# A decoder step on one core: the four output tiles of q made side by side while x and the weights arrive

## The chip, the cores and the metric

The kernel runs on one core of one Trainium2 chip. The metric is device time of one execution in microseconds (us); lower is better. A core has five engines that run beside each other and meet at semaphores: TensorE (PE in the profile, PEld for its weight loads), VectorE (DVE), ScalarE (ACT), GpSimd (POOL) and SyncE (SP, which here only issues transfers). ScalarE and GpSimd can issue transfers too.

## What is computed

One layer of a hybrid decoder, for 256 prompt tokens and 32 sample tokens (N = 288 columns). Cut to what matters here:

```python
def rms_norm(x, g):
    return x * rsqrt(mean(x * x, axis=-1) + EPS) * g

z = rms_norm(x, ln1) @ w_in                   # 288 x 1024 times 1024 x 2560
u, va, q, k, vb = split(z, ...)               # 512 columns each
q = rms_norm(q.reshape(8 heads, 64), q_norm)  # k likewise
mix = concat(spatial_gate(u, va), block_sparse_attention(q, k, vb, paged cache))
h = x + mix @ w_out
h = h + square(relu(rms_norm(h, ln2) @ w_up)) @ w_down
y = h + sigmoid(rms_norm(h, ln3) @ w_ple_gate) * rms_norm(p @ w_ple_proj, ple_norm)
```

The row factor of the first `rms_norm`, 1/sqrt(mean of squares), is called `r1` below. It is a factor per token, so the kernel multiplies it in after the matrix product.

## The kernel before

All activations lie with features on the 128 partitions and the 288 tokens along the free axis. A weight matrix comes as chunks of 128 x 1024 floats (512 KB). In the input projection a chunk holds one output tile: eight blocks of 128 x 128, one for each k, the 128 input features that a block contracts over. Chunks 0 to 3 make q, 4 to 7 k, 8 to 11 v, 12 to 15 u, 16 to 19 a.

Every product is made in three passes of a reduced format (`mm3`, lines 220 to 223). ScalarE rounds a weight to `hi` (line 132), VectorE makes the rest `lo` = raw - hi (line 139); x goes the same way into `Ah` (ScalarE, line 230) and `Al` (VectorE, line 231, an operation on h and Ah with ln1 as a scalar). The passes are hi Ah (L221), hi Al (L222) and lo Ah (L223). A chunk is 8 k times 3 passes, 24 matrix products. There are four buffers for raw chunks and three for `hi` and for `lo`: chunk c+4 is loaded when `lo` of c is done, and chunk c+3 can be rounded when TensorE has done with c.

At the start SP loads x in four pieces of two k each and the first chunks. TensorE begins with nine products of ones that nobody reads (line 296). Then chunk 0 goes over all eight k, then chunk 1, and so on. The squares of x for `r1` are two GpSimd products, two ScalarE squares, one GpSimd sum and three VectorE sums (lines 330 to 341); a product with ones (`stat`, line 235) sums them over the partitions, and `rsqrt_act`, `rsqrt_dve` make `r1` of it. Each tile of q leaves PSUM by a multiplication with `r1` (line 375), is squared (line 377), summed by heads (L235 again) and scaled.

The program text gives an order by turns (`ORDER`, `step`): in a turn w a chunk is used, in a turn T a tile of the paged cache. Such a tile is eight pages of 256 KB. For the first two tiles all eight are issued by SP. A turn T of the first kind multiplies q with the keys of one tile: 16 small products of 32 output rows (line 543). A scheduler then fixes each engine's order ahead of time, so the text's order is not kept to the letter: key products are put between products of chunks. On the chip every engine keeps its fixed order and waits where something is late.

Of the kernel before, what the change touches and what calls it, by code (L numbers as in the profile page):

```python
# [10 lines left out]
AF = mybir.ActivationFunctionType  # L11
# [3 lines left out]
N = 288  # L15
# [20 lines left out]

# w: next chunk of weights, T: next tile of cached pages, G: group of the spatial gate, A: head pair of the prompt's
# attention, m: masks, P: input of the layer embedding, s and S: stores, -: a turn without matrix products of its own
ORDER = (
    "w w w w - w w w m T T T w w w w w w w w T w w - w w w T - T G G s T G A G T w T T T A A - A - T w - "  # L40
    "T T w w T T P w S w w w w w"
# [4 lines left out]
def tile_decode_step(ctx: ExitStack, tc: tile.TileContext, w, xT, pT, kT, vP, pt, vec, const, aws, abd, abs_,  # L46
# [27 lines left out]

# [1 line left out]
    pt_sb = stile([1, 64], "pt", dt=I32)  # L76
# [7 lines left out]
    pool.dma_start(pt_sb, pt)  # L84
    act.dma_start(vec_sb, vec)
    dve.memset(ones, 1.0)
# [19 lines left out]

# [1 line left out]
    h = stile([128, 8, N], "h")  # L108
# [5 lines left out]

# [1 line left out]
    NW = w.shape[0]  # L116
    raw, hi, lo = {}, {}, {}

    def load_w(c, parts=1):
        if c >= NW or c in raw:  # L120
            return
        raw[c] = stile([128, 1024], "raw", NRAW)
        n = 1024 // parts
        for i in range(parts):
            sp.dma_start(raw[c][:, n * i:n * i + n], w[c][:, n * i:n * i + n])
# [16 lines left out]

    # pages are asked for at the pace of the arithmetic, so that weights don't queue behind them
    pace = {"pe": 0.0, "dma": 0.0, "page": 0, "used": 0, "w": 6, "split": 2, "wn": 0}

# [17 lines left out]

# [1 line left out]
    pending = []  # L165
# [14 lines left out]
    def step(unit=None, weights=None, us=2.95):  # L180
        """One turn of the pipeline. A generator that yields n goes on n turns later, with those that read PSUM;
        n + 0.5: with those that need PE, after them; 0: at the end of this turn."""
        if weights is not None:
            pace["wn"] = weights
            for c in range(pace["split"], weights + 1):
                load_w(c)
                split_hi(c)
                split_lo(c)
                pace["split"] = c + 1
        ahead = [c for c in range(pace["split"], pace["wn"] + 3) if c in raw]  # L190
        for c in ahead:
            split_hi(c)
            pace["split"] = c + 1
        for q in pending:
            q[0] = max(q[0] - 1, 0)
        due(0)
        due(1)
        if unit is not None:
            resume(unit)
        for c in ahead:  # L200
            split_lo(c)
        # the second half of w_out waits for the last page
        for c in range(pace["w"], pace["split"] + NRAW):
            if c in raw or c >= NW:
                pace["w"] = c + 1
            elif c < W_HOLD or pace["page"] >= PAGE_HOLD:
                load_w(c)
                pace["w"] = c + 1
                pace["dma"] += 1.46
            else:  # L210
                break
        load_pages(us)
        due(2)
# [4 lines left out]

# [1 line left out]
    def mm3(out, wh, wl, xh, xl, start, stop):  # L220
# [4 lines left out]
    def split(dh, dl, src, scale=None):  # L225
        if scale is None:
            act.activation(dh, src, AF.Copy)
            dve.tensor_tensor(dl, src, dh.bitcast(F32), OP.subtract)
        else:
            act.activation(dh, src, AF.Copy, scale=scale)  # L230
            dve.scalar_tensor_tensor(dl, src, scale, dh.bitcast(F32), OP.mult, OP.subtract)  # L231
# [6 lines left out]
    def rsqrt_act(ss, count):  # L238
        """first guess of 1/sqrt(ss/count + eps), its square, and -(ss/count + eps)/2"""
        y, v, y2 = tmp(), tmp(), tmp()  # L240
        act.activation(y, ss, AF.Abs_reciprocal_sqrt, bias=eps, scale=1.0 / count)
        act.activation(v, ss, AF.Identity, bias=heps, scale=-0.5 / count)
        act.activation(y2, y, AF.Square)
        return y, v, y2
# [5 lines left out]
    def g_rstd(name, acc):  # L250
        t = rsqrt_act(stat(acc, ones), D)
        yield 0
        st[name] = stile([128, N], "rs", 2)
        rsqrt_dve(st[name], *t)
# [9 lines left out]

# [1 line left out]
    def load_x(i):  # L266
        sp.dma_start(h[:, 2 * i:2 * i + 2], xT[:, 2 * i:2 * i + 2])

    load_x(0)
    load_w(0, 2)  # L270
    load_x(1)
    load_x(2)
    load_x(3)
    load_w(1, 2)
    load_w(2)
    load_w(3)
    sp.dma_start(cst, const)
# [5 lines left out]

    def split_x(i):
        for k in range(2 * i, 2 * i + 2):
            split(Ah[:, k], Al[:, k], h[:, k], ln1(k))

    def split_w(c, parts=1):
        n = 1024 // parts
        for i in range(parts):  # L290
            split_hi(c, n * i, n * i + n)
            split_lo(c, n * i, n * i + n)

    warm = misc_ps()
    for _ in range(NWARM):
        pe.matmul(warm[:, 0:128], lhsT=ones, rhs=ones, start=True, stop=True)
    split_x(0)
    split_w(0, 2)
    split_x(1)
    split_x(2)  # L300
    split_x(3)
    load_w(4)
    split_w(1, 2)
    load_w(5)

# [1 line left out]
    def load_p():  # L307
# [21 lines left out]

    def g_x():  # L330
        sq = [sqx[i // 2][:, 2 * (i % 2):2 * (i % 2) + 2] for i in range(4)]
        for i in range(4):
            x = h[:, 2 * i:2 * i + 2]
            if i < 2:
                pool.tensor_tensor(sq[i], x, x, OP.mult)
            else:
                act.activation(sq[i], x, AF.Square)
        pool.tensor_tensor(sq[0], sq[0], sq[1], OP.add)
        dve.tensor_tensor(sq[2], sq[2], sq[3], OP.add)
        dve.tensor_tensor(sq[0], sq[0], sq[2], OP.add)  # L340
        dve.tensor_tensor(xacc, sq[0][:, 0], sq[0][:, 1], OP.add)
        yield 1.5
        yield from g_rstd("r1", xacc)

    resume(g_x())

    def g_embed():
# [15 lines left out]

# [1 line left out]
    def in_tile(c, name, tag):  # L365
# [5 lines left out]
    def u_qk(c, name, tag, g):  # L371
        p = k8(c, Ah, Al, s_ps() if c == 1 else None)
        yield 3 if c == 0 else 2
        j, dst = in_tile(c, name, tag)
        dve.tensor_tensor(dst, p, st["r1"], OP.mult)
        sq = tmp()
        act.activation(sq, dst, AF.Square)
        yield 2.5 if c in (2, 3) else 1.5
        t = rsqrt_act(stat(sq, blk), 64)
        yield 0  # L380
        r = tmp()
        rsqrt_dve(r, *t)
        dve.scalar_tensor_tensor(dst, dst, g, r, OP.mult, OP.mult)
        if name == "q":
            for hh in range(2):
                pp = slice(64 * hh, 64 * hh + 64)
                src = dst[pp, NP:N].rearrange("p (b q) -> p b q", b=8)
                if hh:
                    act.activation(Qb[pp, j, :, :, 2 * j + hh], src, AF.Copy)
                else:  # L390
                    dve.tensor_copy(Qb[pp, j, :, :, 2 * j + hh], src)

    def nat(src, dst_p, dst_s):
        """src [128 feat, 288 tokens] -> dst_p [128 tokens, 2, 128 feat], dst_s [32 tokens, 128 feat]"""
        p = misc_ps()
        for c in range(2):
            pe.transpose(p[:, 128 * c:128 * c + 128], src[:, 128 * c:128 * c + 128], ident)  # L397
        pe.transpose(p[0:NS, 256:384], src[:, NP:N], ident)
        act.activation(dst_p, p[:, 0:256].rearrange("p (c f) -> p c f", c=2), AF.Copy)
        act.activation(dst_s, p[0:NS, 256:384], AF.Copy)  # L400
# [51 lines left out]

# [1 line left out]
    def u_g(g):  # L454
# [17 lines left out]

# [1 line left out]
    def u_A(j):  # L474
# [56 lines left out]

# [1 line left out]
    def u_K(t):  # L533
# [98 lines left out]

# [1 line left out]
    def u_out(c, half, i):  # L634
# [27 lines left out]

# [1 line left out]
    mask_r = stile([128, 256], "maskr", dt=F32R)  # L664
# [22 lines left out]

    wn, kn, cnt = 0, 0, {"G": 0, "A": 0}
    for op in ORDER:
# [21 lines left out]

# [1 line left out]
    hid = []  # L713
# [151 lines left out]
```

## Time and profile before

| | us |
|---|---|
| median of 3 executions | 427.66 (427.47 to 428.17) |
| span of the profiled execution, first to last instruction | 425.1 |
| median minus span: what lies around the span | 2.5 |
| TensorE busy in the span | 414.2 (97%) |
| VectorE, ScalarE, GpSimd busy | 270.0, 206.9, 41.5 |

The profile gives one execution on one core, by its span; the executions that were timed are longer by what lies before the first and after the last instruction. Busy time of TensorE includes the modelled end of each product, so products that follow each other overlap: one lasts 0.29 us, but the next starts after 0.13 us. Times in the rows below count from the start of the span. L12 is line 12 of the kernel, and buffer numbers are left out of names: `raw`, `hi`, `lo` as above, `h` is x, `mm`, `S` and `misc` are PSUM tiles, `T` are shared work tiles, `kv` are cache pages.

### The profile page before, as it was taken

To read this page: it belongs to the slowest core of one execution; us is meant where nothing else is said; L and a number is where in the kernel's file an instruction comes from. 1 tells how busy PE (TensorE), PEld (TensorE's weight loads), DVE (VectorE), ACT (ScalarE), POOL (GpSimd) and SP (SyncE) were. 2 spreads that over 40 slices of the span, in tenths; PEclk is the share of its full clock that TensorE was granted. 3 is DMA by queue.
4 is the path that set the end of the run, shared out by engine and by line. 5 is a ranking of instruction groups with operands and counts; after the bars stand their busy time and mean duration, and the time that the engine had idled before them with its cause. 6 is when DMAs were issued, how large, how long until landed. Compare 5 with 4: busy or idle time off the path is not lost.

```text
span 425.1 us, 8557 instructions
## 1 busy us (share of the span) xinstructions
PE 414.2 (97%) x3100; PEld 371.2 (87%) x3100; DVE 270.0 (64%) x485; ACT 206.9 (49%) x370; POOL 41.5 (10%) x65
## 2 busy tenths in 40 slices
PE   5999999999999999998999999999999999999995
PEld 4997869893575584998999999999999999999995
DVE  4788434657546563597999978777435445435773
ACT  6587325767252353666555445444333343343631
POOL 5401211103113220041000000000000000000000
PEclk9899999999999999999999999999999999999999
DMA  8999994888899688943454545445445455455411
GB/s 269 323 307 351 395 392 158 284 294 306 295 310 311 219 283 310 324 161 126 172 170 154 173 155 188 154 159 188 150 166 180 150 168 178 147 183 167 159 47 56
DMA packets 33963, 92.29 MB, mean 217 GB/s; under 512 B 4753, under 2 KB 6049, under 8 KB 33921
## 3 DMA queue, kind: packets, MB, share of 16 engines
q1 hardware_dynamic: 28944, 77.52, 52.6%
q0 software_dynamic: 3824, 12.34, 8.1%
q10 hardware_dynamic: 1152, 1.89, 1.3%
q8 instruction: 24, 0.39, 0.4%
q14 instruction: 19, 0.15, 0.1%
HBM read 89.31 MB, written 2.42 MB: 216 GB/s over the span
## 4 chain that ended last, share of the span: by engine, by line
PE 93%; DVE 3%; DMA 1%; issue 1%; ACT 1%; SPq 0%; DVEq 0%
PE mm L221 24%; PE mm L222 24%; PE mm L223 24%; PE S L543 5%; PE S L615 4%; PE misc L235 2%; PE misc L480 1%; DMA h<-xT 1%; PE misc L527 1%; DVE T L231 1%; DVE lo L139 1%; PE misc L516 1%; PE misc L483 1%; PE misc L397 1%; PE misc L458 1%
## 5 line engine op out<-in xcount | busy, mean ns | idle before, releaser
L132 ACT ACTIVATE hi<-raw 128x1024 fp32r<-128x1024 f32 (+1 forms) x104 | 108.4, 1043 | 131.2 <-PE mm L222 104.1
L139 DVE TENSOR_TENSOR lo<-raw,hi 128x1024 fp32r<-128x1024 f32 (+1 forms) x104 | 125.0, 1202 | 59.9 <-ACT hi L132 58.2
L221 PE MATMUL mm<-T,hi 128*128 128x288 f32 x296 | 87.9, 298 | 0.2 <-ACT T L230 0.2
L222 PE MATMUL mm<-T,hi 128*128 128x288 f32 x296 | 86.7, 293 | 1.2 <-DVE T L231 1.2
L221 PE MATMUL mm<-Ah,hi 128*128 128x288 f32 x280 | 85.9, 307 | 1.5 <-ACT Ah L230 0.8
L223 PE MATMUL mm<-T,lo 128*128 128x288 f32 x296 | 86.8, 294 | 0.0
L222 PE MATMUL mm<-Al,hi 128*128 128x288 f32 x280 | 84.8, 303 | 1.9 <-DVE Al L231 1.9
L223 PE MATMUL mm<-Ah,lo 128*128 128x288 f32 x280 | 83.6, 299 | 0.4 <-DVE lo L139 0.4
L221 PE MATMUL mm<-kv,hi 128*128 128x288 f32 x224 | 66.1, 295 | 0.0
L222 PE MATMUL mm<-kv,hi 128*128 128x288 f32 x224 | 66.0, 295 | 0.0
L223 PE MATMUL mm<-kv,lo 128*128 128x288 f32 x224 | 65.9, 294 | 0.0
L222 PEld LDWEIGHTS mm<-Al,hi 128*128 128x128 f32 x280 | 53.3, 190 | 5.7 <-issue 3.1
L221 PEld LDWEIGHTS mm<-Ah,hi 128*128 128x128 f32 x280 | 53.1, 190 | 5.2 <-issue 2.9
L222 PEld LDWEIGHTS mm<-T,hi 128*128 128x128 f32 x296 | 55.6, 188 | 1.6 <-DVE T L231 1.5
L221 PEld LDWEIGHTS mm<-T,hi 128*128 128x128 f32 x296 | 55.5, 188 | 0.5 <-ACT T L230 0.4
L223 PEld LDWEIGHTS mm<-T,lo 128*128 128x128 f32 x296 | 55.4, 187 | 0.0
L223 PEld LDWEIGHTS mm<-Ah,lo 128*128 128x128 f32 x280 | 53.3, 190 | 1.7 <-issue 1.0
L222 PEld LDWEIGHTS mm<-kv,hi 128*128 128x128 f32 x224 | 42.3, 189 | 0.0
L223 PEld LDWEIGHTS mm<-kv,lo 128*128 128x128 f32 x224 | 42.3, 189 | 0.0
L221 PEld LDWEIGHTS mm<-kv,hi 128*128 128x128 f32 x224 | 42.0, 188 | 0.0
L543 PE MATMUL S<-kv,T 128*32 128x256 f32 x256 | 24.3, 384 | 0.0
L736 DVE TENSOR_TENSOR tmp<-mm,rs 128x288 f32<-128x288 f32 x32 | 14.6, 456 | 10.8 <-PE mm L223 10.7
(193 smaller groups left out, 446.8 us busy)
## 6 DMA issues: line engine op xcount, KB each, us to landing
raw<-w SPq DMA_DIRECT2D x100, 512.0 KB, 3.3
kv<-kT SPq DMA_DIRECT2D x46, 256.0 KB, 4.8
kv<-vP SPq DMA_DIRECT2D x31, 256.0 KB, 4.5
kv<-vP POOLq DMA_DIRECT2D x27, 256.0 KB, 5.5
kv<-kT POOLq DMA_DIRECT2D x18, 256.0 KB, 5.5
kv<-vP ACTq DMA_DIRECT2D x6, 256.0 KB, 5.2
h<-xT SPq DMA_DIRECT2D x4, 288.0 KB, 5.2
raw<-w SPq DMA_DIRECT2D x4, 256.0 KB, 5.3
```

What stands on the lines that cost most here:

```text
L132: act.activation(hi[c][:, a:b], raw[c][:, a:b], AF.Copy)
L139: dve.tensor_tensor(lo[c][:, a:b], raw[c][:, a:b], hi[c][:, a:b].bitcast(F32), OP.subtract)
L221: pe.matmul(out, lhsT=wh, rhs=xh, start=start, stop=False)
L222: pe.matmul(out, lhsT=wh, rhs=xl, start=False, stop=False)
L223: pe.matmul(out, lhsT=wl, rhs=xh, start=False, stop=stop)
L231: dve.scalar_tensor_tensor(dl, src, scale, dh.bitcast(F32), OP.mult, OP.subtract)
L235: pe.matmul(p[:, :N], lhsT=lhsT, rhs=src, start=True, stop=True)
L397: pe.transpose(p[:, 128 * c:128 * c + 128], src[:, 128 * c:128 * c + 128], ident)
L458: pe.matmul(p[:, 128 * c:128 * c + 128], lhsT=an[:, 128 * c:128 * c + 128], rhs=aws_sb[:, g, :], start=True, stop=True)
L543: pe.matmul(S[32 * b:32 * b + 32, c0:c0 + 256].rearrange("p (j s) -> p j s", j=2), lhsT=Qbd[:, q0:q0 + 32], rhs=kt[:, b, :, j, :], start=j ...
L615: pe.matmul(O[32 * b:32 * b + 32, :], lhsT=PT[:, c:c + 32], rhs=vt[:, v0:v0 + 512], start=False, stop=n == 3 and j == 1, tile_position=(0, ...
L736: dve.tensor_tensor(t, p, st["r2"], OP.mult)
```

## The change

x comes in five pieces (k 0; k 1; k 2, 3; k 4, 5; k 6, 7). The first four are issued by ScalarE, the last by SP behind the chunks 0 to 3; the small vector with ln1 goes from ScalarE's queue to the head of SP's. The host lays chunks 0 to 3 out anew: each now holds two k for all four tiles of q, so the tiles are made together, in four PSUM tiles, two k per chunk, and all of q is done when the last chunk is. The squares of x and their sums are seven GpSimd operations, but for one last sum on VectorE. `r1` is summed by TensorE right behind the last product of q. Four turns w and one empty turn leave `ORDER`, and eight chunks are asked for ahead instead of six.

```diff
-    "w w w w - w w w m T T T w w w w w w w w T w w - w w w T - T G G s T G A G T w T T T A A - A - T w - "
+    "w w w m T T T w w w w w w w w T w w - w w w T - T G G s T G A G T w T T T A A - A - T w - "
...
-    act.dma_start(vec_sb, vec)
+    sp.dma_start(vec_sb, vec)
...
-    load_x(0)
+    def load_x(eng, a, b):
+        eng.dma_start(h[:, a:b], xT[:, a:b])
+
+    load_x(act, 0, 1)
     load_w(0, 2)
-    load_x(1)
-    load_x(2)
-    load_x(3)
+    load_x(act, 1, 2)
+    load_x(act, 2, 4)
+    load_x(act, 4, 6)
     load_w(1, 2)
-    load_w(2)
-    load_w(3)
+    load_w(2, 2)
+    load_w(3, 2)
+    load_x(sp, 6, 8)
     sp.dma_start(cst, const)
...
+    qp = [s_ps(), s_ps(), mm_ps(), mm_ps()]
+    for c in range(4):
+        for i in range(2):
+            k = 2 * c + i
+            split(Ah[:, k], Al[:, k], h[:, k], ln1(k))
+            split_hi(c, 512 * i, 512 * i + 512)
+            split_lo(c, 512 * i, 512 * i + 512)
+            for j in range(4):
+                s = slice(512 * i + 128 * j, 512 * i + 128 * j + 128)
+                mm3(qp[j][:, :N], hi[c][:, s], lo[c][:, s], Ah[:, k], Al[:, k], k == 0, k == 7)
+        sq = sqx[c // 2][:, 2 * (c % 2):2 * (c % 2) + 2]
+        x = h[:, 2 * c:2 * c + 2]
+        pool.tensor_tensor(sq, x, x, OP.mult)
+        if c:
+            pool.tensor_tensor(sqx[0][:, 0:2], sqx[0][:, 0:2], sq, OP.add)
+        load_w(4 + c)
+    dve.tensor_tensor(xacc, sqx[0][:, 0], sqx[0][:, 1], OP.add)
+    for _ in g_rstd("r1", xacc):
+        pass
...
-        p = k8(c, Ah, Al, s_ps() if c == 1 else None)
-        yield 3 if c == 0 else 2
+        p = qp[c][:, :N] if c < 4 else k8(c, Ah, Al)
+        yield 1
...
-    head = np.concatenate([chunks(c, 8, 128) for c in cols] + [chunks(wo[:512], 4, 256), chunks(wo[512:], 4, 256)])
+    head = np.concatenate([chunks(cols[0], 2, 512)] + [chunks(c, 8, 128) for c in cols[1:]] + [chunks(wo[:512], 4, 256), chunks(wo[512:], 4, 256)])
```

What this does to the fixed orders is shown at three places. The first is GpSimd from its first clearing of a work tile to the loads of the gate's weights; `T_20`, `T_21` are the tiles of the squares, `pt` is the page table. Before:

```order
L111 MEMSET T_13_79 128x1152
L335 ISA
L335 TENSOR_TENSOR T_20_98<-h_77 128x576 x2
L158 TENSOR_LOAD pt_61
L158 ISA x2
L338 TENSOR_TENSOR T_20_98<-T_20_98 128x576
L668 DMA aws_64<-aws 128x512
```

With the change:

```order
L302 ISA
L302 TENSOR_TENSOR T_20_101<-h_77 128x576 x2
L302 TENSOR_TENSOR T_21_102<-h_77 128x576
L304 TENSOR_TENSOR T_20_101<-T_20_101 128x576
L302 TENSOR_TENSOR T_21_102<-h_77 128x576
L304 TENSOR_TENSOR T_20_101<-T_20_101,T_21_102 128x576
L158 TENSOR_LOAD pt_61
L158 ISA x2
L304 TENSOR_TENSOR T_20_101<-T_20_101,T_21_102 128x576
L655 DMA aws_64<-aws 128x512
```

Three operations of 128 x 576 have become seven: four squares and three sums.

The second place is VectorE over the same stretch. Before:

```order
L231 SCALAR_TENSOR_TENSOR Al_97<-h_77,vec_62,Ah_96 128x288 x2
L139 TENSOR_TENSOR lo_117<-raw_82,hi_115 128x512 x2
L231 SCALAR_TENSOR_TENSOR Al_97<-h_77,vec_62,Ah_96 128x288 x6
L139 TENSOR_TENSOR lo_137<-raw_88,hi_135 128x512 x2
L339 TENSOR_TENSOR T_21_99<-T_21_99 128x576
L139 TENSOR_TENSOR lo_189<-raw_91,hi_154 128x1024
```

With the change (chunk 0 and the first half of chunk 1; it goes on so up to k 7):

```order
L231 SCALAR_TENSOR_TENSOR Al_100<-h_77,vec_62,Ah_99 128x288
L139 TENSOR_TENSOR lo_122<-raw_82,hi_120 128x512
L231 SCALAR_TENSOR_TENSOR Al_100<-h_77,vec_62,Ah_99 128x288
L139 TENSOR_TENSOR lo_122<-raw_82,hi_120 128x512
L231 SCALAR_TENSOR_TENSOR Al_100<-h_77,vec_62,Ah_99 128x288
L139 TENSOR_TENSOR lo_159<-raw_88,hi_157 128x512
```

For each k there is now one `Al` and one half chunk of `lo`, sixteen operations up to the end of q.

The third place is TensorE where the first tile of cache pages (`kv_193` before, `kv_340` with the change) is multiplied. Before, behind chunk 6:

```order
L223 MATMUL mm_582<-Ah_96,lo_479 128x288
L235 MATMUL misc_647<-tmp_572,const_63 128x288
L543 MATMUL S_655<-kv_193,T_13_79 32x256 x16
L235 MATMUL misc_714<-tmp_645,const_63 128x288
L235 MATMUL misc_774<-tmp_707,const_63 128x288
L221 MATMUL mm_838<-Ah_96,hi_503 128x288
```

With the change the same sixteen are spread over chunks 6 to 8; this is the end of chunk 7 (`mm_814`) and the start of chunk 8 (`mm_848`):

```order
L222 MATMUL mm_814<-Al_100,hi_351 128x288
L530 MATMUL S_575<-kv_340,T_13_79 32x256 x5
L223 MATMUL mm_814<-Ah_99,lo_398 128x288
L221 MATMUL mm_814<-Ah_99,hi_351 128x288
L222 MATMUL mm_814<-Al_100,hi_351 128x288
L223 MATMUL mm_814<-Ah_99,lo_398 128x288
L530 MATMUL S_575<-kv_340,T_13_79 32x256 x4
L235 MATMUL misc_682<-tmp_565,const_63 128x288
L221 MATMUL mm_848<-Ah_99,hi_434 128x288
L222 MATMUL mm_848<-Al_100,hi_434 128x288
L530 MATMUL S_575<-kv_340,T_13_79 32x256 x4
L223 MATMUL mm_848<-Ah_99,lo_488 128x288
```

Key products stand in 26 unbroken runs in the whole program with the change, in 23 before.

## Rows read from the trace of the kernel before

**Rows 1.** TensorE's waits: line, releaser: us in total, times, longest.

```profile
PE mm L222 <- DVE Al L231: 1.9, 2, 0.9
PE mm L222 <- DVE T L231: 1.2, 1, 1.2
```

**Rows 2.** Stretches: engines' busy us (instructions), granted clock, DMA share, GB/s.

```profile
8.00:10.00 2.00, 1.01 (x4) 0.61 (x4) 1.97 (x3) 2.00 (x6) 1.92 (x2) 1.00 1.06 404
12.00:14.00 2.00, 2.00 (x10) 2.00 (x9) 2.00 (x5) 1.28 (x2) 0.22 (x1) 0.50 1.04 421
24.00:180.00 156.00, 156.00 (x1196) 115.38 (x1195) 88.61 (x206) 79.58 (x185) 24.38 (x45) 1.00 0.86 303
```

**Rows 3.** TensorE in order of time (start, us): q's first product, `r1`, q's end.

```profile
5.54 0.40 PE L221 MATMUL mm<-Ah,hi 128*128 128x288 f32 x1 [0.65 <-ACT hi L132]
...
20.18 0.65 PE L235 MATMUL misc<-tmp,ones 128*128 128x288 f32 x2
...
24.26 0.29 PE L222 MATMUL mm<-Al,hi 128*128 128x288 f32 x1
24.39 0.30 PE L223 MATMUL mm<-Ah,lo 128*128 128x288 f32 x1
```

**Rows 4.** GpSimd in order of time, 7 to 11 us.

```profile
7.53 1.49 POOL L335 TENSOR_TENSOR T<-h 128x576 f32<-128x576 f32 x1 [2.49 <-DMA h<-xT]
9.10 1.51 POOL L338 TENSOR_TENSOR T<-T 128x576 f32<-128x576 f32 x1
```

**Rows 5.** VectorE in order of time, 7 to 14 us.

```profile
7.33 0.69 DVE L139 TENSOR_TENSOR lo<-raw,hi 128x512 fp32r<-128x512 f32 x1 [0.94 <-ACT hi L132]
...
8.05 1.28 DVE L231 SCALAR_TENSOR_TENSOR Al<-h,vec,Ah 128x288 fp32r<-128x288 f32 x1
...
9.26 1.67 DVE L231 SCALAR_TENSOR_TENSOR Al<-h,vec,Ah 128x288 fp32r<-128x288 f32 x1
...
10.85 1.79 DVE L231 SCALAR_TENSOR_TENSOR Al<-h,vec,Ah 128x288 fp32r<-128x288 f32 x4
12.57 1.28 DVE L139 TENSOR_TENSOR lo<-raw,hi 128x512 fp32r<-128x512 f32 x2
```

**Rows 6.** The transfer of chunk 3: its issue on SP, and time to landing.

```profile
L125 SPq DMA_DIRECT2D raw<-w x1: 691/691/691, 5.3 to 5.3; - x1
...
DMA to landing us min/median/max: 7.3/7.3/7.3
```

**Rows 7.** VectorE and ScalarE behind `r1`'s sum: q's first tile out, its square.

```profile
23.11 0.46 DVE L375 TENSOR_TENSOR T<-mm,rs 128x288 f32<-128x288 f32 x1
...
23.60 0.81 ACT L377 ACTIVATE tmp<-T 128x288 f32<-128x288 f32 x2 [0.56 <-DVE T L375]
```

**Rows 8.** TensorE around one key product alone, and around thirteen.

```profile
42.33 0.29 PE L221 MATMUL mm<-Ah,hi 128*128 128x288 f32 x1
42.55 0.62 PE L543 MATMUL S<-kv,T 128*32 128x256 f32 x2
...
43.34 0.30 PE L223 MATMUL mm<-Ah,lo 128*128 128x288 f32 x1
...
61.87 0.29 PE L221 MATMUL mm<-Ah,hi 128*128 128x288 f32 x1
62.09 1.91 PE L543 MATMUL S<-kv,T 128*32 128x256 f32 x26
...
64.17 0.29 PE L223 MATMUL mm<-Ah,lo 128*128 128x288 f32 x1
```

**Rows 9.** SP at the first tile's eighth page, and TensorE at that tile.

```profile
26.05 0.34 SPq L160 DMA_DIRECT2D kv<-kT  x1
...
36.64 1.93 PE L543 MATMUL S<-kv,T 128*32 128x256 f32 x32
```

**Rows 10.** GpSimd's masking of the gate's weights; VectorE at the same time.

```profile
15.25 3.08 POOL L671 TENSOR_SCALAR_AFFINE_SELECT aws<-aws 128x512 f32<-128x512 f32 x1 [3.02 <-DMA aws<-aws]
...
16.24 1.22 DVE L139 TENSOR_TENSOR lo<-raw,hi 128x1024 fp32r<-128x1024 f32 x1
```

More of the change, by code (lines that the diff above doesn't have):

```diff
@@ L141, in tile_decode_step @@
     kvt = {}
-    pace = {"pe": 0.0, "dma": 0.0, "page": 0, "used": 0, "w": 6, "split": 2, "wn": 0}
+    pace = {"pe": 0.0, "dma": 0.0, "page": 0, "used": 0, "w": 8, "split": 4, "wn": 0}
     def load_pages(us, tile_needed=-1):
@@ L263, in k8 @@
         return p[:, :N]
-    def load_x(i):
-        sp.dma_start(h[:, 2 * i:2 * i + 2], xT[:, 2 * i:2 * i + 2])
-    load_x(0)
+    def load_x(eng, a, b):
+        eng.dma_start(h[:, a:b], xT[:, a:b])
+    load_x(act, 0, 1)
     load_w(0, 2)
-    load_x(1)
-    load_x(2)
-    load_x(3)
+    load_x(act, 1, 2)
+    load_x(act, 2, 4)
+    load_x(act, 4, 6)
     load_w(1, 2)
-    load_w(2)
-    load_w(3)
+    load_w(2, 2)
+    load_w(3, 2)
+    load_x(sp, 6, 8)
     sp.dma_start(cst, const)
@@ L282, in tile_decode_step @@
     xacc = tmp()
[L284 to L292, printed above, removed]
     warm = misc_ps()
@@ L296, in tile_decode_step @@
         pe.matmul(warm[:, 0:128], lhsT=ones, rhs=ones, start=True, stop=True)
[L297 to L304, printed above, removed]
+    qp = [s_ps(), s_ps(), mm_ps(), mm_ps()]
[17 more added lines that the diff above has]
+        pass
     def load_p():
@@ L328, in u_ple @@
                     act.activation(e[:, 4 * i + jj], ps[jj][:, :N], AF.Copy)
[L330 to L345, printed above, removed]
     def g_embed():
@@ L686, in u_w @@
         return u_out(c, half, i)
-    wn, kn, cnt = 0, 0, {"G": 0, "A": 0}
+    for c in range(4):
+        resume(u_w(c))
+    wn, kn, cnt = 4, 0, {"G": 0, "A": 0}
     for op in ORDER:
```

## Prediction, written before the changed kernel ran

> **What bounds the kernel now.** I read the table first: TensorE is busy 97% of the span. That share is no proof that it sets the end, so the waits came second: behind the start TensorE waits 1.2 us for `T` and otherwise 1.9 us for `Al`, which is at the start [rows 1]. Third the stretches: from 24 to 180 us TensorE is busy for all of 156 us, with the transfers' engines at 0.86 and VectorE at little more than half [rows 2]. So whatever the fixed order adds to TensorE there is added to the time, and a gain at the start comes through only as far as TensorE reaches the end of q earlier. Fourth the order of time: TensorE's first product of q starts at 5.54, its last, the 96th, at 24.39, and plain products follow every 0.13 us; so q is done at 24.5, with the sum for `r1` (20.18, about half a us) inside [rows 3]. Without that sum it is 24.0. 96 products need 12.8 us of the 18.5: between 8 and 10 us TensorE starts only four, while VectorE is busy throughout, and between 12 and 14 ten, at a granted clock of 0.50, the lower of the two levels (1.2 GHz) [rows 2]. At the start VectorE is late, not the weights: this is where the change works.
>
> **The change part by part.** *Two k per chunk.* TensorE can begin each k when two `Ah`, `Al` and half a chunk are there, 12 products or 1.6 us per k. Data don't prevent that: chunk 3, before, is the last of x and the four chunks and lands at 5.3 + 7.3 = 12.6 us [rows 6]. The same bytes now end with x's last pair, so it lands near 12.6 too. ScalarE's queue takes x but the transfers' engines are full already (share 1.06 [rows 2]), so the split over two queues reorders arrivals and costs ScalarE three issues; I count nothing for it.
>
> *VectorE.* Up to the end of q it has one `Al` and one half `lo` per k. Undisturbed, four `Al` take 1.79 us, a start every 0.43, and two half `lo` 1.28 [rows 5]: 1.07 us per k, less than TensorE's 1.6.
>
> *GpSimd.* Here lies the price. A square was dispatched at 7.53 and ended at 9.02; VectorE's `lo` had ended at 8.02, so the square ran 1.00 us from there. An `Al` dispatched at 8.05 ended at 9.33, 0.31 behind the square; GpSimd's sum ended at 10.61, 1.28 us behind that `Al`; the `Al` dispatched at 9.26 ended at 10.93, 0.32 behind the sum [rows 4, 5]. The two engines took turns, each waiting for the other's whole instruction; `Al` took 1.28 and 1.67 us where 0.51 is its time alone. Seven GpSimd operations now cost 4 x 1.00 + 3 x 1.28 = 7.8 us of turns, three of them behind x's last pair: 12.6 + 0.3 (an `Al` in between) + 1.0 + 0.5 + 1.3 + 0.3 + 1.3 = 17.3 us, with one VectorE operation between two of them. Counted so, VectorE stands at the half `lo` of k 4 then and ends it at 17.8. From there TensorE is the slower one: ten products left of k 4 and three k, 1.3 + 4.8 us, end q at 23.9. From below: fifteen VectorE operations behind the first product, 8.1 us, and 7.8 of GpSimd, end `lo` of k 7 at 21.4, less some overlap, and ten products later q at 22.3. I take 23.7, near the first sum, because the last three GpSimd operations can't start before 12.6. Against 24.0 that is **-0.3 us**, ends -2 and +1. The low clock can return: between 8 and 18 us only some 12 products run per 3 us. At 0.50, two us hold ten products instead of fifteen [rows 2], so three or four us cost 1.0 to 1.3; I take none, since VectorE's waits would hide most of it.
>
> The notes on the chip bear on one thing here. The masking of the gate's weights on GpSimd ran from 15.25 to 18.33 and a whole `lo` beside it took 1.22 [rows 10], not more than two halves alone (1.28). The Trainium skill (SBUF — State Buffer, section Who interferes with whom) states that a VectorE instruction with two SBUF inputs contends with a GpSimd instruction that reads SBUF, for the whole instruction. For squares and sums the rows say the same; for the masking they don't. By the rule the masking, now behind the sums, would also hold VectorE at the steps to `r1` and the sum below would be about 0.5 us higher; by the rows it holds nothing, and I go by the rows.
>
> *`r1` behind q.* From the start of its sum (20.18) to q's first tile leaving PSUM (23.11) and its square's end (23.60 + 0.41) pass 3.8 us [rows 3, 7]; TensorE had 29 products to go on with. Now the sum stands behind q's last product, and behind it chunk 4 alone, 24 products or 3.2 us, before the head sum that needs that square. With the sum's own half us that is 3.7 against 3.8, and ScalarE has the rounding of chunk 6 ahead of its first step, whose buffer q's last product frees: up to 0.5 more. All of TensorE's queue stands behind that head sum. A second, small wait follows at q's second tile, six products on. **+0.6 us**, ends 0.1 and 1.2.
>
> *Key products in more runs.* One key product alone stands between products that start at 42.33 and 43.34, 1.01 us apart where two steps take 0.27; thirteen make it 2.30 [rows 8]. So one more product in a run costs 1.29 / 12 = 0.11, and a run of its own 1.01 - 0.27 - 0.11 = 0.63 us. The order has 26 runs instead of 23, and TensorE has no idle time there to hide it [rows 2]: **+1.9 us**, ends 1.3 (one of the runs stands where TensorE waits anyway) and 2.5 (before the first value tile it is 15 instead of 11).
>
> *Cache pages.* Before, the first tile's eighth page is issued at 26.05 and its keys are multiplied at 36.64 [rows 9], 10.6 us later. Now SP takes the loads of chunks 4 to 8 ahead of the first page and chunk 12 ahead of the last two, and that load waits for `lo` of chunk 8. My estimate is that the eighth page lands within a us of its use. I count 0, up to +1.5. What else SP issues is gated by `lo` and moves with it.
>
> Sum: -0.3 + 0.6 + 1.9 + 0 = **+2.2 us** on the span of 425.1, so 427.3; the median lies 2.5 above the span, and 427.66 + 2.2 = **429.9 us**.
>
> **The rivals.** *Faster: GpSimd doesn't hold VectorE up at the start.* Place: k 0 to 7. If `Al` and `lo` run at 0.51 and 0.68, TensorE goes from 5.5 through 96 products, with some 0.4 of waits for the first `lo`, and ends q at 18.7, 5.3 us earlier; the other two terms stay, -5.3 + 2.5 = -2.8, **424.9 us**. For it: two of the three operations before ran where VectorE had little else to do. Against it: every `Al` that met one waited to its end [rows 4, 5]. It decides once q ends before 21.5, where 24.0 less the other terms' 2.5 is even.
>
> *No change: the turns cost less.* x's first pieces land early enough for four GpSimd operations to be over before 12.6 while VectorE keeps ahead; q ends near 22, -2.0, `r1` costs little and the runs 1.9: **427.7 us**. For it: the lower end above. Against it: the three late operations.
>
> *Slower still: pages and clock.* The five key products inside chunk 7 wait for the eighth page, and the clock falls while TensorE is bound: +2.2 + 1.5 + 1.2 gives **432.6 us**. For it: SP's order, and the low stretch before; against it: both can hide.
>
> **How the numbers follow.** The forecast has 0.45 and, by its terms' ends taken singly, its own range is 428.6 to 431.2. Faster has 0.17, no change 0.23, slower still 0.15. A difference of 0.2%, 0.86 us, is about what a measurement of this kernel tells from none. Faster by more than that, below 426.8: 0.17 and a little of the second case, 0.20. Within: 0.20. Slower: 0.60. The range 425.2 to 432.5 leaves out about the fast half of the first rival and the slow half of the third.
>
> **What would show it.** GpSimd has seven operations back to back from about 7 to 17 us, of 1.0 to 1.5 us, and `Al` beside them takes over 1 us. TensorE has bursts of twelve products with gaps up to 18 us, and q's last product starts near 23.6. A gap of about half a us follows chunk 4, before the head sum. A key product alone among chunk products shows 1.01 us again. If q ends before 21.5 with `Al` at 0.5, the forecast is wrong in its first term; if TensorE waits for `kv`, in the fourth.

## Result, and the profile after

The change made the kernel slower: 433.25 us (median of 7 executions, 431.60 to 433.77) against 428.17 us before (7 executions beside them, 427.12 to 430.77); ratio 1.0104, 95% interval 1.0070 to 1.0138. The forecast was 429.9 with a range up to 432.5: the direction was right, the size too small (2.2 us where 5.1 were measured). The profiled execution has a span of 432.2 us, 7.1 more than before, and 1.6 us lie around it instead of 2.5, so the span overstates the loss; the terms below are worked out on the spans. Two kernels below (x on one queue; the kernel before, pages early) had one execution each at a lower granted clock, 0.847 and 0.974, which their times and ratios leave out, while the profile of the second is of that execution.

The first view after is again TensorE's waits (line, releaser: us in total, times, longest).

```profile
PE S L223 <- DVE lo L139: 4.0, 5, 1.3
PE S L602 <- DMA kv<-vP: 1.4, 1, 1.4
...
PE misc L235 <- ACT tmp L364: 0.9, 1, 0.9
```

Where [rows 1] had 1.9 us for `Al` there are 4.0 us for `lo` now, still at the start. The other two are new: 0.9 at the head sum behind chunk 4, which the prediction had at 0.6, and 1.4 for a page of a value tile, which it had at nothing. The stretches of [rows 2], after:

```profile
8.00:10.00 2.00, 1.61 (x10) 1.36 (x11) 1.81 (x2) 2.00 (x5) 1.65 (x2) 1.00 1.05 402
12.00:14.00 2.00, 1.67 (x12) 1.44 (x11) 2.00 (x2) 0.67 (x3) 2.00 (x2) 1.00 0.86 340
24.00:180.00 156.00, 153.64 (x1153) 109.99 (x1152) 86.97 (x204) 76.96 (x180) 26.04 (x47) 1.00 0.87 300
```

The clock kept its full level at the start, where it had been at 0.50 before. Between 24 and 180 us TensorE got through 1153 products where it had done 1196: the loss is there, at a busy share of 98%. GpSimd and VectorE at the start, in order of time, show why the start gained nothing ([rows 4, 5] before):

```profile
8.35 2.86 POOL L302 TENSOR_TENSOR T<-h 128x576 f32<-128x576 f32 x2 [5.13 <-DMA h<-xT]
...
12.73 1.63 POOL L304 TENSOR_TENSOR T<-T 128x576 f32<-128x576 f32 x1
14.31 1.60 POOL L302 TENSOR_TENSOR T<-h 128x576 f32<-128x576 f32 x1
15.87 3.46 POOL L304 TENSOR_TENSOR T<-T,T 128x576 f32<-128x576 f32 x2
```

```profile
8.19 0.69 DVE L139 TENSOR_TENSOR lo<-raw,hi 128x512 fp32r<-128x512 f32 x1 [1.26 <-ACT hi L132]
8.80 1.40 DVE L231 SCALAR_TENSOR_TENSOR Al<-h,vec,Ah 128x288 fp32r<-128x288 f32 x1
10.13 1.63 DVE L139 TENSOR_TENSOR lo<-raw,hi 128x512 fp32r<-128x512 f32 x1
11.68 1.40 DVE L231 SCALAR_TENSOR_TENSOR Al<-h,vec,Ah 128x288 fp32r<-128x288 f32 x1
...
17.97 1.68 DVE L231 SCALAR_TENSOR_TENSOR Al<-h,vec,Ah 128x288 fp32r<-128x288 f32 x1
19.57 0.68 DVE L139 TENSOR_TENSOR lo<-raw,hi 128x512 fp32r<-128x512 f32 x1
20.17 0.51 DVE L231 SCALAR_TENSOR_TENSOR Al<-h,vec,Ah 128x288 fp32r<-128x288 f32 x1
```

Seven GpSimd operations stand back to back from 8.35 to 19.33 us, and exactly one VectorE operation falls between two of them. An `Al` takes 1.40 to 1.68 there and 0.51 afterwards, half a `lo` 1.63 to 1.90 and then 0.68. That is the mechanism that was forecast, 2 us longer. TensorE around the end of q (start, us) and behind chunk 4:

```profile
24.78 0.29 PE L223 MATMUL mm<-Ah,lo 128*128 128x288 f32 x1
24.91 0.65 PE L235 MATMUL misc<-tmp,ones 128*128 128x288 f32 x2
...
28.46 0.29 PE L223 MATMUL mm<-Ah,lo 128*128 128x288 f32 x1
29.65 0.75 PE L235 MATMUL misc<-tmp,const 128*128 128x288 f32 x2 [0.90 <-ACT tmp L364]
```

q ends at 24.91; without its sum it had ended at 24.0 before [rows 3]. Then the pages: SP's queue, and TensorE's key products of the first tile (start, us).

```profile
24.87 0.36 SPq L160 DMA_DIRECT2D kv<-kT  x1
...
32.97 1.47 SPq L160 DMA_DIRECT2D kv<-kT  x2
36.72 0.34 SPq L125 DMA_DIRECT2D raw<-w  x1
37.85 6.42 SPq L160 DMA_DIRECT2D kv<-kT  x6
```

```profile
38.66 0.62 PE L530 MATMUL S<-kv,T 128*32 128x256 f32 x2
39.89 0.62 PE L530 MATMUL S<-kv,T 128*32 128x256 f32 x4
43.31 1.05 PE L530 MATMUL S<-kv,T 128*32 128x256 f32 x10
45.01 0.64 PE L530 MATMUL S<-kv,T 128*32 128x256 f32 x8
46.52 0.64 PE L530 MATMUL S<-kv,T 128*32 128x256 f32 x8
```

The eighth page is the second of the six from 37.85 on; the trace puts its issue at 39.42 and its landing at 42.61, 13.4 us later than the issue before [rows 9]. And the sixteen products that stood together from 36.64 [rows 9] are scattered over 8 us. All 256 records of key products by line (busy us, mean ns, idle before):

```profile
L530 PE MATMUL S<-kv,T 128*32 128x256 f32 x256 | 26.3, 385 | 0.0
L602 PE MATMUL S<-kv,PT 128*32 128x512 f32 x128 | 18.1, 598 | 1.4 <-DMA kv<-vP 1.4
```

Before, the first of these groups was busy for 24.3 us:

```profile
L543 PE MATMUL S<-kv,T 128*32 128x256 f32 x256 | 24.3, 384 | 0.0
```

At matched products the two traces lie apart by +0.4 us at the last product of q, +5.3 at the first value product (97.08 and 102.42), +6.9 at the 65th value product (159.85 and 166.72; the wait for the value page lies between, at 112 us) and +6.7 at the last products. From 228 us to the last product nothing is lost or gained; the last 0.4 of the 7.1 lie behind it.

### The profile page after: what moved, and what is told of

Its sections match the earlier page's. It is cut to its first block, busy times and chain, and to the rows that moved or that the text cites. A ratio compares the mean times of both kernels' runs of the same rounds, so it can differ in the third digit from the quotient of the medians.

```text
span 432.2 us, 8576 instructions
## 1 busy us (share of the span) xinstructions
PE 417.6 (97%) x3100; PEld 371.0 (86%) x3100; DVE 273.4 (63%) x485; ACT 206.0 (48%) x370; POOL 48.3 (11%) x69
## 4 chain that ended last, share of the span: by engine, by line
PE 87%; DVE 3%; DMA 3%; issue 1%; ACT 1%; SPq 1%; DVEq 0%; ACTq 0%
PE mm L221 23%; PE mm L223 23%; PE mm L222 23%; PE S L530 6%; PE S L602 3%; DMA kv<-vP 2%; PE misc L235 1%; PE misc L467 1%; DMA raw<-w 1%; DVE lo L139 1%; PE misc L514 1%; DVE T L231 1%; PE misc L470 1%; PE misc L503 1%; PE misc L445 1%
## 5 line engine op out<-in xcount | busy, mean ns | idle before, releaser
L139 DVE TENSOR_TENSOR lo<-raw,hi 128x1024 fp32r<-128x1024 f32 (+1 forms) x106 | 128.7, 1215 | 66.2 <-ACT hi L132 64.1
L221 PE MATMUL mm<-Ah,hi 128*128 128x288 f32 x272 | 83.7, 308 | 0.0
L223 PE MATMUL mm<-Ah,lo 128*128 128x288 f32 x272 | 81.4, 299 | 0.0
L222 PE MATMUL mm<-Al,hi 128*128 128x288 f32 x272 | 80.9, 298 | 0.0
L221 PEld LDWEIGHTS mm<-Ah,hi 128*128 128x128 f32 x272 | 51.1, 188 | 5.2 <-issue 4.7
L223 PEld LDWEIGHTS mm<-Ah,lo 128*128 128x128 f32 x272 | 51.2, 188 | 3.0 <-issue 2.9
L222 PEld LDWEIGHTS mm<-Al,hi 128*128 128x128 f32 x272 | 51.1, 188 | 1.5 <-issue 1.2
L530 PE MATMUL S<-kv,T 128*32 128x256 f32 x256 | 26.3, 385 | 0.0
```

The source lines that it names most:

```text
L139: dve.tensor_tensor(lo[c][:, a:b], raw[c][:, a:b], hi[c][:, a:b].bitcast(F32), OP.subtract)
L221: pe.matmul(out, lhsT=wh, rhs=xh, start=start, stop=False)
L222: pe.matmul(out, lhsT=wh, rhs=xl, start=False, stop=False)
L223: pe.matmul(out, lhsT=wl, rhs=xh, start=False, stop=stop)
L530: pe.matmul(S[32 * b:32 * b + 32, c0:c0 + 256].rearrange("p (j s) -> p j s", j=2), lhsT=Qbd[:, q0:q0 + 32], rhs=kt[:, b, :, j, :], start=j ...
```

## Experiments

Two theories stood after the result. Theory 1: the turns of VectorE and GpSimd keep the start from gaining. Theory 2: the pages are late, because the planner asks for them by a clock of arithmetic (`pace["pe"]`) to which every turn adds, and the change took four turns w (2.95 us each) and an empty one (0.5) out of `ORDER`. Late pages then scatter the key products in the planned order and make TensorE wait. Rivals: only the start matters, or only the weights do. In the figures below a run of key products is a row of them between two other products in TensorE's planned order.

**Squares on ScalarE.**

```diff
-        pool.tensor_tensor(sq, x, x, OP.mult)
+        act.activation(sq, x, AF.Square)
         if c:
-            pool.tensor_tensor(sqx[0][:, 0:2], sqx[0][:, 0:2], sq, OP.add)
+            dve.tensor_tensor(sqx[0][:, 0:2], sqx[0][:, 0:2], sq, OP.add)
```

> The changed kernel with the four squares of x on ScalarE and their sums on VectorE; nothing is left for GpSimd there. Theory 1 (turns of VectorE and GpSimd set the end of q): Al beside it falls from 1.40 to 0.51 us and half a lo from 1.6-1.9 to 0.68, q's last product starts at 19.5 to 20.5 instead of 24.78, and the time falls by as much, from 433.25 to about 428.5, since TensorE is busy behind it. Rival (what comes behind q waits for late cache pages anyway, so a gain at the start is given back there): q ends as early, but TensorE waits or its key products are spread more, and the time stays at 432 to 433. Second rival (the weights and x set the pace): q ends at 23 or later, 432 to 433.

Measured: 431.69 us, 1.0107 of before (1.0025 to 1.0190), so its time can't be told from the changed kernel's; span 430.4. q's last product starts at 20.60, as theory 1 says, 4.2 us earlier. At the first value product 4.1 us are left of it (98.31 against 102.42), at the last products 1.8: what is lost is lost among the value tiles, in another planned order (27 runs of key products, and 1.1 us of waits for `kv`). For the time, the first rival holds, but not by the means that it named: those waits stand at 48 and 52 us, ahead of the first value product, and key products are busy for 25.8 us, less than in the changed kernel.

**The planner's clock credited.**

```diff
-    pace = {"pe": 0.0, "dma": 0.0, "page": 0, "used": 0, "w": 8, "split": 4, "wn": 0}
+    pace = {"pe": 9.4, "dma": 0.0, "page": 0, "used": 0, "w": 8, "split": 4, "wn": 0}
```

> The changed kernel with one number altered: the planner's clock of the arithmetic starts at 9.4 us instead of 0, what the four chunks of q gave it before (four turns of 2.95 and one of 0.5, less two chunk loads of 1.46). SP then issues the first tile's eighth page behind chunk 10's load instead of chunk 12's, and key products stand in 22 runs instead of 26 (11 instead of 15 before the first value tile). Theory 2 (late pages cost what is not explained by the start): the wait of 1.4 for kv at a value tile goes, and the key products cost some 3 us less; 433.25 - 4.4 = about 428.9. Theory by the prediction's own price of 0.63 per run: 4 x 0.63 = 2.5 less, 430.7. Rival (only the start matters): no change, 433. q's end stays at 24.8 in each.

Measured: 428.19 us, 1.0013 of before (0.9970 to 1.0055), 5.1 us less than the changed kernel by one number (3.9 by the two ratios, each to the kernel before run beside it; 5.3 by the spans). TensorE's waits in this run, and its key products by line:

```profile
PE S L223 <- DVE lo L139: 3.7, 4, 1.4
PE misc L235 <- ACT tmp L364: 1.3, 1, 1.3
...
PE S L221 <- ACT hi L132: 0.8, 1, 0.8
```

```profile
L530 PE MATMUL S<-kv,T 128*32 128x256 f32 x256 | 22.8, 384 | 0.0
L602 PE MATMUL S<-kv,PT 128*32 128x512 f32 x128 | 18.1, 598 | 0.0
```

The 1.4 us for the value page are gone, and key products are busy for 22.8 us instead of 26.3. These two make 4.9 of the 5.3 us between the spans (432.2 and 426.9). q's last product starts at 24.49, 0.3 earlier. The pages are early again: counted in order of landing, they land 4.6 to 20 us later in the changed kernel than before (10 us in the middle), and with the credit 1.6 us later in the middle. Theory 2 is confirmed, and the rival "only the start" has fallen.

**Both.** The two edits together.

> Both edits together: squares on ScalarE, sums on VectorE, and the planner's clock credited with 9.4 us. Key products stand in 23 runs (10 before the first value tile). If the two causes add up: 433.25 - 4.7 - 4.4 = 424.2, faster than the kernel before (428.2) by 4.0. If the pages set the pace behind the start: no faster than the credit alone, 428 to 429. If the start alone matters: as squares on ScalarE alone, 428.5.

Measured: 428.64 us, 1.0028 (0.9993 to 1.0063): no better than the credit alone, though q's last product starts at 21.09. The gain of 3.4 us is still 3.7 at the first value product (94.99 against 98.68), and is lost between 137 and 162 us: from the 225th record of a key product to the 65th of a value product this kernel takes 21.7 us (140.32 to 162.00), the one with the credit alone 18.0 (143.48 to 161.52). The small products there stand in another planned order, with more changes between kinds; which edit to the order did it was not tried. Squares on ScalarE alone loses in the same stretch (4.9 us ahead of the changed kernel at the 225th key product, 1.2 at the 65th value product). The causes did not add up.

**The kernel before, pages late.**

```diff
-    pace = {"pe": 0.0, "dma": 0.0, "page": 0, "used": 0, "w": 6, "split": 2, "wn": 0}
+    pace = {"pe": -9.4, "dma": 0.0, "page": 0, "used": 0, "w": 6, "split": 2, "wn": 0}
```

> The kernel before with one number altered the other way: the planner's clock of the arithmetic starts at -9.4 us. Pages stand where the change puts them (the first behind chunk 8's load, the eighth behind chunk 12's), and key products stand in 26 runs instead of 23, 15 instead of 11 before the first value tile. q is made as before, its end at 24.4. Theory 2: key products cost 2.5 to 3.5 us more and a value or key tile waits some 1 to 1.5: 428.2 + 4.4 = 432.6. By the prediction's price alone, 3 x 0.63 = 1.9 more: 430.1. If where the key products stand costs nothing: 428.2.

Measured: 434.71 us, 1.0182 (1.0109 to 1.0255). The old start, with late pages alone, costs as much as the whole change; that it costs more isn't clear of the noise of four executions. The rows by line:

```profile
L543 PE MATMUL S<-kv,T 128*32 128x256 f32 x256 | 26.5, 384 | 2.0 <-DMA kv<-kT 2.0
L615 PE MATMUL S<-kv,PT 128*32 128x512 f32 x128 | 17.8, 598 | 0.0
```

2.2 us more of key products than before and 2.0 of waiting; at the first value product the run lies 6.2 us behind the kernel before, the changed kernel 5.3. The 4.2 are what these rows show; no row names the other 2 us.

**Pages first.** In the loop of q, behind each chunk load:

```diff
         load_w(4 + c)
+        pace["dma"] += 1.46 * (c > 1)
+        load_pages(2.2)
```

> The changed kernel in which the planner is asked for pages inside the loop of q already, behind each chunk load, with 2.2 us of arithmetic credited each time. All eight pages of the first tile stand ahead of chunk 6's load on SP's queue instead of behind chunk 12's, and key products stand in 21 runs (9 before the first value tile) where the changed kernel has 26 (15) and the credit alone 22 (11). Theory 2 (late pages and the key products that they scatter): no wait for kv, key products cheaper than with the credit by 0.7 to 1.3, so 428.2 - 1 = about 427. Rival (pages ahead of the weights make chunks 5 to 8 late): TensorE waits for hi or lo behind q and the time is 430 or more. q's end stays at 24.5 to 25.

Measured: 427.58 us, 1.0016 (0.9996 to 1.0036). Key products are busy for 22.2 us, 0.6 less than with the credit; q's last product starts at 24.84. The time is within 0.6 us of theory 2's, but the kernel before ran 0.8 us faster beside it (426.87 against 427.68): by the ratios, 1.0016 and 1.0013, the gain of 1 us over the credit did not show, and only the spans (426.1 and 426.9) have it. The rival has fallen: behind q TensorE waits for a weight 0.4 us at most.

**Pages first, squares on ScalarE.** Both diffs above, which leave TensorE's order as in pages first, instruction for instruction.

> The same with the squares of x on ScalarE and their sums on VectorE; the order of TensorE's products is that of the run with pages first alone. q's end at about 20.6 instead of 24.8. Since the order is the same, this tells whether a gain at the start comes through: if it does (the rest is TensorE's own work), the time is 4 us below that of pages first alone, 423 to 424. If weights or pages land too late for the earlier start, TensorE waits for hi, lo or kv and half or more of the 4 us is lost: 425.5 to 427.

Measured: 423.98 us, 0.9932 of before (0.9901 to 0.9964): faster than both kernels. VectorE at the start, in order of time:

```profile
12.94 0.52 DVE L231 SCALAR_TENSOR_TENSOR Al<-h,vec,Ah 128x288 fp32r<-128x288 f32 x1 [0.15 <-ACT Ah L230]
13.46 0.69 DVE L139 TENSOR_TENSOR lo<-raw,hi 128x512 fp32r<-128x512 f32 x1
...
15.10 0.75 DVE L304 TENSOR_TENSOR T<-T,T 128x576 f32<-128x576 f32 x1
...
16.99 0.52 DVE L231 SCALAR_TENSOR_TENSOR Al<-h,vec,Ah 128x288 fp32r<-128x288 f32 x1
17.42 0.69 DVE L139 TENSOR_TENSOR lo<-raw,hi 128x512 fp32r<-128x512 f32 x1
```

`Al` and `lo` run at their own 0.52 and 0.69, q's last product starts at 20.28 instead of 24.84, and of these 4.6 us 3.7 are left in the span (422.4 and 426.1). With pages in time and the order held still, the start's gain comes through: theory 1 in its clean form.

**The kernel before, all squares on GpSimd.** One part of the change alone, `g_x`:

```diff
-            if i < 2:
-                pool.tensor_tensor(sq[i], x, x, OP.mult)
-            else:
-                act.activation(sq[i], x, AF.Square)
-        pool.tensor_tensor(sq[0], sq[0], sq[1], OP.add)
-        dve.tensor_tensor(sq[2], sq[2], sq[3], OP.add)
-        dve.tensor_tensor(sq[0], sq[0], sq[2], OP.add)
+            pool.tensor_tensor(sq[i], x, x, OP.mult)
+            if i:
+                pool.tensor_tensor(sq[0], sq[0], sq[i], OP.add)
```

> The kernel before with one part of the change alone: all four squares of x and their three running sums on GpSimd. Key products stand in 24 runs instead of 23. Theory 1 (VectorE and GpSimd take turns, about 1.0 to 1.3 us each): Al and lo beside them take over 1.2 us, and q, which needs all of Al, ends 1.5 to 3 us later than 24.4; the time is 430 to 431. Rival (VectorE has room there, or the squares fall behind its work): q ends within 0.5 of 24.4, 428.2 to 429.

Measured: 433.16 us, 1.0166 (1.0111 to 1.0222), more than theory 1 had. Its stretches:

```profile
10.00:12.00 2.00, 1.27 (x5) 0.76 (x4) 2.00 (x3) 1.78 (x3) 2.00 (x3) 0.50 1.03 412
14.00:18.00 4.00, 3.25 (x12) 2.55 (x12) 4.00 (x5) 0.89 (x1) 3.64 (x5) 0.50 0.14 17
```

q's last product starts at 27.81, 3.4 later. VectorE is held, TensorE starts twelve products in four us, and the granted clock stands at 0.50, the level of 1.2 GHz, from 10 to 18 us, where the kernel before had it there from 11.0 to 14.4. How much of the 3.4 us is the clock's was not told apart. The other 2.6 us come later, in an order that has moved as well. The rival that VectorE has room has fallen.

**x on one queue.** x's five pieces back on SP, `vec` on ScalarE (`load_x(act, ...)` to `load_x(sp, ...)`).

> The changed kernel with x's five pieces back on SP's queue between the weights, and vec on ScalarE's. The planned order moves with it: the first page now stands behind chunk 10's load and key products stand in 28 runs (16 before the first value tile). If the two queues do nothing but reorder arrivals, as the prediction had it, x's last pair still lands at 13 to 14 and q's end stays within 0.5 of 24.8; if the second queue brings x early, q ends 1 to 2 us later. In both cases the later pages and two more runs of key products should cost 1 to 2 us: 434 to 435.5, by theory 2.

Measured: 439.10 us, 1.0270 (1.0226 to 1.0314), 3.6 us above the upper end of what was expected. x's last pair lands at 13.53 instead of 13.34, so the second queue does only reorder arrivals; but the plan puts five `Al` ahead of a `lo`, TensorE waits 4.2 us for one `lo`, the granted clock stands at 0.50 from 14 to 18 us, and q's last product starts at 25.96. Key products stand in 28 runs, busy for 27.7 us, and 6.4 of the 13.8 us on the span appear only behind the first value product. The edit moved the whole plan, so it says little of the queue.

**Sums on VectorE.** Pages first with the squares on GpSimd and the three sums on VectorE; TensorE's order unchanged.

> Pages first, with the four squares on GpSimd and the three sums on VectorE; TensorE's order is the same instruction for instruction as in pages first and in pages first with squares on ScalarE. Theory 1 counts turns: four GpSimd operations instead of seven at the start, so some 4/7 of the 4.56 us between the ends of q in these two (24.84 and 20.28): q's end at 22.9, and since the end follows it, 424.0 + 2.6 x 0.8 = about 426. Rival (the sums, which read two tiles, are what holds VectorE, squares hardly): q's end under 21.5 and 424 to 424.5. Second rival (any GpSimd operation there costs as much, since the sums now lengthen VectorE's own chain): q's end at 24 or more, 427.5.

Measured: 427.12 us, 0.9990 (0.9962 to 1.0018). q's last product starts at 21.50: three GpSimd operations less gave 3.3 of the 4.6 us, more than their share by count. The time hardly moved: the sum for `r1`, right behind q in TensorE's order, waits 0.8 us for VectorE's last sum, and key products wait 1.3 us for `kv`, which neither of the other two runs in this order does by more than 0.2:

```profile
PE S L532 <- DMA kv<-kT: 1.3, 2, 1.0
...
PE misc L235 <- DVE tmp L308: 0.8, 1, 0.8
```

The step from q's end to the time failed here: the sum for `r1` starts at 22.61, 2.1 us behind the run with the squares on ScalarE, and with 1.1 us more of waits for `kv` that is 3.2 us, where the spans (425.5 and 422.4) lie 3.1 apart.

**The kernel before, pages early.** `pace["pe"]` starts at 9.

> The kernel before with the planner's clock of the arithmetic started at 9 us: all sixteen pages of the first two tiles stand behind chunk 6's load (before: the eighth behind chunk 8's, the sixteenth behind chunk 11's), and key products stand in 16 runs instead of 23, 6 instead of 11 before the first value tile. Nothing else is altered; q ends at 24.4. Theory 2 (what scattered key products cost is added to the time): 7 runs at 0.63 less, 427.5 - 4.4 = 423. Rival (pages ahead of chunk 7 to 9 make the weights late): TensorE waits for hi or lo and at least 2 us of that is lost: 425.5 or more.

Measured: 434.26 us, 1.0120 (1.0040 to 1.0201): the rival, and worse. Key products are busy for 21.5 us instead of 24.3, but chunk 7's load is issued at 37.14, behind all sixteen pages, and TensorE stands:

```profile
PE mm L221 <- ACT hi L132: 4.7, 3, 4.2
```

How the rest came about stays open.

**More pages ahead of chunk 5.** Pages first with squares on ScalarE, and `pace["pe"]` starting at 3, then at 6.

> Pages first with squares on ScalarE and sums on VectorE, the planner's clock started at 3 us on top: the first tile's eight pages stand ahead of chunk 5's load, key products in 19 runs instead of 21 (8 instead of 9 before the first value tile). Theory 2: 2 x 0.63 less than pages first with squares on ScalarE, 424.0 - 1.2 = 422.8. Rival (chunk 5 too late behind the pages): TensorE waits for hi or lo after q and the time is 424 to 426.

> The same with the clock started at 6 us: fourteen pages stand ahead of chunk 5's load, key products in 16 runs. Theory 2 alone: 5 x 0.63 less than pages first with squares on ScalarE, 420.8. By the rows of that run, chunk 5 then lands about 14 x 0.65 = 9 us later than chunk 4, at some 26, and its lo is ready at 28 to 29 while q and chunk 4 are done at 24.2: TensorE waits for 3 to 4 us, less what key products fill, so about 423 to 425. If it is under 422, weights aren't the limit there.

Measured: 426.85 us (0.9977, 0.9941 to 1.0013) and 429.35 us (1.0037, 1.0005 to 1.0069). Both are behind the 423.98, though key products stand in fewer runs; for the first the intervals of the ratios still overlap (0.9932 has 0.9901 to 0.9964), so only the second is clearly worse: in the first TensorE waits 2.8 us for `hi` at chunk 5, in the second it starts 20 products between 26 and 30 us:

```profile
26.00:30.00 4.00, 2.43 (x20) 1.03 (x18) 2.75 (x8) 1.43 (x5) 0.00 (x0) 1.00 0.89 293
```

So pages can also be too early, for the weights: of the places tried, the first tile's ahead of chunk 6 has the lowest time.

## Why the prediction was too low

*Turns at the start*: right in kind, but the term was 1.2 us too small. Counted was -0.3 against 24.0, measured +0.9. The price per GpSimd operation held: the second square ended at 11.21, 1.01 us behind the `Al` that ended at 10.20, the first sum at 14.36, 1.28 behind the `Al` that ended at 13.08. What was left out for the first four is VectorE's own part of each turn (half a `lo` ended at 11.76, 0.55 behind the square), and the first square started at 8.35, not near 7. So four operations were not over when x's last pair landed (at 13.34, not 12.6), and the seventh ended at 19.33 instead of 17.3.

*`r1` behind q*: forecast 0.6, measured 0.9, in the place that was named.

*Key products in more runs*: right. Three more runs, priced at 0.63 each, gave 1.9; by line it is 26.3 - 24.3 = 2.0. Up to the first value product there are four more runs and key products cost 2.7 us more (14.7 instead of 12.0), behind it one fewer and 0.6 less. Over the kernels the price holds roughly, with some up to 0.8 us off a straight line (squares on ScalarE alone has 27 runs and 25.8 us) and the kernel before with pages early further off (16 runs in its plan, 21.5 us):

| kernel | runs | busy us |
|---|---|---|
| pages first, squares on ScalarE, clock from 6 | 16 | 20.3 |
| pages first, with and without squares on ScalarE | 21 | 22.2 |
| clock credited | 22 | 22.8 |
| kernel before | 23 | 24.3 |
| changed kernel | 26 | 26.3 |
| x on one queue | 28 | 27.7 |

From 16 to 28 runs that is 7.4 / 12 = 0.62 us per run.

*Cache pages* is the step that failed. It counted 0, because the eighth page "lands within a us of its use". For the first tile that held: the page landed at 42.61, and TensorE waited for none of that tile. But the prediction followed SP's queue only to the first tile, and does not speak of what the diff shows: five turns leave `ORDER`, 12.3 us of the clock by which pages are asked for. Every page behind was late too, and the wait of 1.4 stands at a value tile 70 us on. And the extra runs of key products, which the prediction took from the planned order as a separate term, had the same cause: with the clock credited their number falls from 26 to 22, and 4 to 5 us go from the time. Without the late pages the changed kernel lands at 428.19, by its number on the case that was called "no change", but not by its means: q ends at 24.6 there instead of near 22, and key products are 1.5 us cheaper than before.

The sum on the span, measured: +0.9, +0.9, +2.0 and +1.4 make 5.2 of 7.1, where 2.2 were forecast. The pages are 1.4 of what was missed, the turns 1.2, the other two terms 0.4 together, and 1.9 no row names. Of the 5.3 us at the first value product, q's end, the wait at the head sum and key products up to there make 4.5; the rest there is not settled.

*Range and rivals.* The forecast's own range, 428.6 to 431.2, is a little narrower than its terms' ends taken singly (428.2 to 431.4); 433.25 lies outside both. By number "slower still" (432.6) is nearest, by accident: the clock that it had falling stood at 1.00, and the page that it had late for the first tile was not waited for. "GpSimd doesn't hold VectorE up" has fallen in the changed kernel, where every `Al` and half `lo` that fell between two GpSimd operations waited.

*The masking.* From [rows 10] the prediction concluded that the masking holds nothing on VectorE, against the Trainium skill (SBUF — State Buffer, section Who interferes with whom). The runs side with the rule: the two do contend. VectorE's sum `tmp<-T` took 0.45 us in the run with pages first and squares on ScalarE; in the kernel before with all squares on GpSimd it met the masking and took 0.89. VectorE and GpSimd in that kernel, in order of time:

```profile
16.34 3.55 DVE L139 TENSOR_TENSOR lo<-raw,hi 128x512 fp32r<-128x512 f32 x4
19.81 0.89 DVE L337 TENSOR_TENSOR tmp<-T 128x288 f32<-128x288 f32 x1
```

```profile
19.09 1.30 POOL L667 TENSOR_SCALAR_AFFINE_SELECT aws<-aws 128x512 f32<-128x512 f32 x1 [1.37 <-DMA aws<-aws]
```

The masking, 3.08 us in [rows 10], lasted 1.30 here and ended at 20.39, 0.5 us behind the last `lo` (19.89); the sum ended 0.31 behind it. So about 0.5 us of it are its own, and the rest it waited. In the changed kernel the masking alone waited, for three operations, while VectorE went on from one operation to the next:

```profile
22.37 3.08 POOL L658 TENSOR_SCALAR_AFFINE_SELECT aws<-aws 128x512 f32<-128x512 f32 x1 [1.43 <-DMA aws<-aws]
```

```profile
23.37 0.45 DVE L306 TENSOR_TENSOR tmp<-T 128x288 f32<-128x288 f32 x1
23.74 1.22 DVE L139 TENSOR_TENSOR lo<-raw,hi 128x1024 fp32r<-128x1024 f32 x1
```

It ended 0.5 us behind that `lo`, as it had ended 0.5 behind VectorE's last sum in the kernel before (18.33 and 17.83). So [rows 10] were read rightly for that record, in which VectorE was not held; a long record was read as long work, and the conclusion that the masking can hold nothing failed. The 0.5 us that the prediction set aside by the Trainium skill's rule would have been about right as a price for one meeting like that of the sum (0.89 against 0.45); in the changed kernel none fell on the way to `r1`. What decides which of the two waits was not tried.

## What to carry to other kernels

When a change deletes steps from a list, ask what else those steps drove: here five turns were also the clock for prefetching, and that was worth 4 to 5 us, of which 1.4 show as a wait. To learn what an edit at the start is worth, hold the planned order still, as the pair with pages first does; an edit that moves the plan measures the plan. And move a vector engine's helper work to an engine that doesn't take turns with it before the critical stage is regrouped.

## What the hardware showed beyond that

A run of key products of its own costs about 0.62 us over its place in a longer run, by the table above, and it is counted as busy time: TensorE's busy share of 98% hid it. VectorE and GpSimd alternated strictly on the squares and sums of x: for eleven us of the changed kernel's start each held the other for one whole instruction. The masking got no such turn there and waited for three operations of VectorE. And a record of GpSimd can be mostly waiting (3.08 us for 0.5 of masking), which no column of the profile says; where it ends behind VectorE's records shows it.
